# Latent attention in one block: a written-out order, one weight split per pair of heads, and a rotation in three operations

## The chip, the cores and the metric

The kernel runs on one core of a Trainium2 chip. The metric is the device time of one execution in microseconds; the time before is the median of three runs. A core has TensorE (matrix products, into PSUM), VectorE, ScalarE, GpSimd and SyncE, each with a queue of its own that it works off in the order written into the program, and 16 DMA engines that bring the weights from HBM.

## The reference

Three blocks run one after the other on 256 tokens of width 1024: a mixer with attention and a recurrence, a neighbourhood attention with its feed-forward part, and a latent attention with a mixture of 8 experts. The change is in the latent attention of the third (16 heads, 64 plain and 32 rotated columns per query and key, 64 per value):

```python
    down = h @ w_down
    c_q = _rmsnorm(down[..., :MLA_Q_LORA]) * q_norm
    c_kv = _rmsnorm(down[..., MLA_Q_LORA:MLA_Q_LORA + MLA_KV_LORA]) * kv_norm
    k_rope = down[..., MLA_Q_LORA + MLA_KV_LORA:]
    q = (c_q @ w_uq).reshape(B, S, MLA_HEADS, MLA_NOPE + MLA_ROPE)
    kv = (c_kv @ w_ukv).reshape(B, S, MLA_HEADS, MLA_NOPE + MLA_V)
    ...
        s = (jnp.einsum('bqhd,bkhd->bhqk', qn, k_nope)
             + jnp.einsum('bqhr,bkr->bhqk', qr, k_rope)).astype(jnp.float32) * scale
        p = jax.nn.softmax(s, axis=-1).astype(v.dtype)
        return jnp.einsum('bhqk,bkhd->bqhd', p, v)
```

The rotation takes neighbouring columns x1, x2 to x1 cos - x2 sin and x1 sin + x2 cos. Afterwards `w_o` projects the heads' output (the output projection, `out_proj`), a router follows, and then the experts.

## The kernel before

**Precision by splitting.** A matrix operand is split into a high part, which ScalarE casts (`whi`, line 98; `hi` in `split_to`, line 524), and a rest, which VectorE subtracts (`wlo`, line 99; `lo`). TensorE multiplies high by high, high by rest and rest by high: three matmuls for each product (lines 486, 487 and 489 for token-major products, 699 to 701 for scores). I call the subtractions rests. The turned softmax weights and the values are not split (line 676).

**The weight stream.** `Stream` brings raw weights by DMA from SyncE's queue (line 79) into a ring of buffers and splits them (`split`) up to five pieces ahead of their use. `W.next()` hands out the next piece and first splits as many further ones as there is room for.

**The latent attention.** The 16 heads are worked in eight pairs, 0 to 7. For every second pair `prepare` first forms the queries of four heads, a group (twelve matmuls of 384 columns, into two PSUM buffers `pb`), copies them (`qt`, line 1149) and rotates their last 32 columns (`turn`, lines 1068 to 1073, for each half `t` of the tokens). For each pair it then forms the keys (three matmuls of 256 columns, lines 1153 to 1155), transposes the queries (line 1162) and splits both. `scores` multiplies into PSUM buffers `pa`, one for each half of the tokens, both heads side by side. `softmax_rows` takes the maximum (line 643), scales it (644), lets ScalarE exponentiate with the row sums (646), and normalises (648, 650). `turn_P` transposes the weights of a pair (663) and ScalarE copies them back to SBUF (`pt`, 669); `pv` multiplies them with the values (676) and splits the result into `oT`, of which `out_proj` needs one piece of 128 columns for each pair.

**What sets the order.** The program is written pair by pair (`attention`, with preparation two pairs ahead), and a scheduler then lays out each engine's queue by its priorities; instructions of neighbouring pairs, and of the output projection behind them, move between each other. Only in the experts' stage is the written order kept: `in_order` chains the instructions of TensorE, ScalarE and VectorE there. The time of each stage can be read from the timeline: the attention's lead begins near 698 us, its first reduction is at 713, the output projection ends at 783, the experts' first product is at 806.

Of the kernel before, what the change touches and what calls it, by code (L numbers as in the profile page):

```python
# [9 lines left out]
F32 = mybir.dt.float32  # L10
# [4 lines left out]
OP = mybir.AluOpType  # L15
# [13 lines left out]
class Stream:  # L29
# [115 lines left out]

    def flush(self):
# [28 lines left out]
def consts():  # L175
# [8 lines left out]
    rope = np.stack([np.cos(ang), np.sin(ang)], 1).astype(np.float32)  # L184
# [4 lines left out]
def model(ctx: ExitStack, tc: tile.TileContext, A, out, cap=128):  # L189
# [443 lines left out]
    def softmax_rows(Ps, srcs, biases, scale):  # L633
# [4 lines left out]
        for i in range(n):  # L638
            if biases is not None:
                V.tensor_tensor_reduce(Ps[i], srcs[i], biases[i], scale=1.0, scalar=-3.0e38, op0=OP.add, op1=OP.max,  # L640
                                       accum_out=mx[:, i:i + 1])
            else:
                V.tensor_reduce(mx[:, i:i + 1], srcs[i], axis=AX.X, op=OP.max)
        V.tensor_scalar(mx, mx, -scale, None, OP.mult)
        for i in range(n):
            SC.activation(Ps[i], srcs[i] if biases is None else Ps[i], AF.Exp, bias=mx[:, i:i + 1], scale=scale,
                          accum_out=sums[:, i:i + 1])
# [7 lines left out]

    def turn_P(P, pt, causal, rev):
        for h in range(2):
            ps = pbc()
            p3 = ps.rearrange("p (k t n) -> p k t n", k=2, t=2)
            for kt in range(2):  # L660
                for t in range(2):
                    if not (causal and kt > t):
                        PE.transpose(p3[:, kt, t], P[:, t, h, kt * 128:(kt + 1) * 128], ident)
            run = lambda o, i: (o.rearrange("p (m n) -> p m n", n=rev), back(i, rev)) if rev else (o, i)
            if causal:
                V.tensor_copy(*run(pt[:, h, 0], ps[:, 0:256]))
                V.tensor_copy(*run(pt[:, h, 1, 128:256], p3[:, 1, 1]))
            else:
                SC.copy(*run(pt[:, h].rearrange("p k n -> p (k n)"), ps))
# [382 lines left out]
    with ExitStack() as ph:  # L1052
# [5 lines left out]
        rope = p.tile([128, 2, 2, 16], F32, name="rope")  # L1058
# [487 lines left out]
```

## Time and profile before

| | |
|---|---|
| median of three runs | 1327.18 us (1326.76 to 1331.44) |
| the profiled execution | 1326.26 us, span 1324.4 us |
| TensorE | busy 1254.7 us, 95% |
| VectorE | busy 1076.9 us, 81% |
| ScalarE | busy 846.5 us, 64% |
| DMA | 359.56 MB, mean 271 GB/s |

The span is what the profiler's records cover; the execution's own time is 1.9 us longer. A matmul's recorded time overlaps the next one's, so a busy TensorE need not be one at its peak. An engine's idle time costs only where the chain that ends last passes through it.

### The profile page before, as it was taken

The page shows a single profiled execution, that of the slowest core. Times are in us where ns is not written, and L with a number is a line of the kernel's source. Part 1 is how long each engine was busy: PE and PEld are TensorE (multiplying, and loading weights), DVE is VectorE, ACT ScalarE, POOL GpSimd, SP SyncE. Part 2 cuts the span into 40 slices and gives each one's busy share as a digit, 9 for nine tenths or more (in the row PEclk, how much of TensorE's full clock was granted, in tenths as well). Part 3 has the DMA queues.
Part 4 walks back from the last instruction along what each step waited for, and adds up shares of the span by engine and source line. Part 5 has one row for each costly group of instructions (what it writes and reads, how often), then busy time and mean ns, then how long its engine had stood idle before and what let it go on. Part 6 is the DMA issues. An engine that isn't in the chain of part 4 may idle for free. (4 is left out here: it accounts for less than half of the span.)

```text
span 1324.4 us, 20099 instructions
## 1 busy us (share of the span) xinstructions
PE 1254.7 (95%) x7459; PEld 1118.0 (84%) x7459; DVE 1076.9 (81%) x1761; ACT 846.5 (64%) x1354; POOL 37.0 (3%) x68
## 2 busy tenths in 40 slices
PE   6988999999999989999998988999999999999985
PEld 6976989999798779999987667899999889988873
DVE  6796799997897496878768867988888898888976
ACT  7874456555566453434447747788778777878762
POOL 4000000000100000000000020000000000000100
PEclk9988999999899989999979998999999999999987
DMA  9844599892785287899642145999999999999980
GB/s 330 305 143 148 159 384 343 295 315 96 231 259 163 80 307 262 312 382 346 221 138 92 32 138 192 389 372 361 368 385 366 352 381 363 370 357 391 375 320 34
DMA packets 190171, 359.56 MB, mean 271 GB/s; under 512 B 15460, under 2 KB 147970, under 8 KB 189937
## 3 DMA queue, kind: packets, MB, share of 16 engines
q1 hardware_dynamic: 187361, 351.70, 75.1%
q10 hardware_dynamic: 1584, 3.91, 0.8%
q0 software_dynamic: 1120, 2.58, 0.5%
q8 instruction: 61, 1.00, 0.3%
q14 instruction: 45, 0.37, 0.1%
HBM read 351.56 MB, written 7.06 MB: 271 GB/s over the span
## 5 line engine op out<-in xcount | busy, mean ns | idle before, releaser
L99 DVE TENSOR_TENSOR wlo<-raw,whi 128x1024 fp32r<-128x1024 f32 (+2 forms) x577 | 644.5, 1155 | 126.0 <-ACT whi L98 119.0
L98 ACT CAST whi<-raw 128x1024 fp32r<-128x1024 f32 (+2 forms) x577 | 557.7, 1003 | 115.9 <-PE pa L489 30.8
L1467 PE MATMUL pa<-whi,xT 128*128 128x448 f32 x512 | 189.3, 370 | 3.8 <-ACT whi L98 3.8
L1468 PE MATMUL pa<-wlo,xT 128*128 128x448 f32 x512 | 187.0, 365 | 1.7 <-DVE wlo L99 1.7
L1469 PE MATMUL pa<-whi,xT 128*128 128x448 f32 x512 | 186.0, 363 | 0.0
L289 DVE SCALAR_TENSOR_TENSOR acc<-raw,cact,acc 128x1024 f32<-128x1024 f32 x84 | 107.2, 1276 | 2.9 <-DMA raw<-in_w_ada_dram 2.7
L1467 PEld LDWEIGHTS pa<-whi,xT 128*128 128x128 f32 x512 | 96.7, 189 | 11.9 <-ACT whi L98 4.9
L1468 PEld LDWEIGHTS pa<-wlo,xT 128*128 128x128 f32 x512 | 96.8, 189 | 9.4 <-DVE wlo L99 3.1
L1469 PEld LDWEIGHTS pa<-whi,xT 128*128 128x128 f32 x512 | 96.5, 189 | 6.4
L486 PE MATMUL pb<-whi,hTh 128*128 128x512 f32 x224 | 88.4, 395 | 0.7 <-ACT hTh L524 0.7
L487 PE MATMUL pb<-wlo,hTh 128*128 128x512 f32 x224 | 88.4, 395 | 0.1
L478 PE MATMUL pb<-hTh,whi 128*128 128x256 f32 x512 | 74.6, 289 | 1.1 <-ACT hTh L575 0.9
L478 PEld LDWEIGHTS pb<-hTh,whi 128*128 128x128 f32 x512 | 70.3, 196 | 6.0 <-ACT hTh L575 1.6
L478 PE MATMUL pb<-hTl,whi 128*128 128x256 f32 x512 | 72.4, 283 | 0.0
L478 PE MATMUL pb<-hTh,wlo 128*128 128x256 f32 x512 | 71.9, 283 | 0.0
L489 PE MATMUL pb<-whi,hTl 128*128 128x512 f32 x224 | 71.0, 395 | 0.0
L487 PE MATMUL pa<-wlo,fh 128*128 128x512 f32 x176 | 69.2, 393 | 0.6 <-DVE wlo L99 0.6
L486 PE MATMUL pa<-whi,fh 128*128 128x512 f32 x176 | 69.3, 394 | 0.0
L478 PEld LDWEIGHTS pb<-hTl,whi 128*128 128x128 f32 x512 | 66.3, 192 | 0.0
L478 PEld LDWEIGHTS pb<-hTh,wlo 128*128 128x128 f32 x512 | 66.1, 192 | 0.0
L478 PE MATMUL pc<-hTh,whi 128*128 128x256 f32 x448 | 63.8, 285 | 1.2 <-ACT whi L98 1.2
L478 PE MATMUL pc<-hTh,wlo 128*128 128x256 f32 x448 | 63.0, 283 | 0.0
(433 smaller groups left out, 2074.0 us busy)
## 6 DMA issues: line engine op xcount, KB each, us to landing
raw<-in_moe_w_gu_dram SPq DMA_DIRECT2D x128, 896.0 KB, 7.4
raw<-in_moe_w_down_dram SPq DMA_DIRECT2D x56, 1024.0 KB, 6.7
raw<-in_w_ada_dram SPq DMA_DIRECT2D x48, 1024.0 KB, 7.8
raw<-in_w_up_dram SPq DMA_DIRECT2D x22, 1024.0 KB, 9.7
raw<-in_ffn_w_gu_dram SPq DMA_DIRECT2D x22, 1024.0 KB, 6.2
raw<-in_na_w_qkv_dram SPq DMA_DIRECT2D x12, 1024.0 KB, 5.1
raw<-in_w_down_dram SPq DMA_DIRECT2D x11, 1024.0 KB, 4.8
raw<-in_ffn_w_down_dram SPq DMA_DIRECT2D x11, 1024.0 KB
```

The source lines that it names most:

```text
L98: self.last = self.nc.scalar.copy(h, src)
L99: self.nc.vector.tensor_sub(l, src, h.bitcast(F32))
L289: V.scalar_tensor_tensor(ada_acc[0], raw, cact[:, k:k + 1], ada_acc[0], op0=OP.mult, op1=OP.add)
L478: PE.matmul(ps, lhsT=w[:, k], rhs=x[:, k], start=n + k == 0, stop=n == 2 and k == KD - 1)
L486: PE.matmul(acc[t][j][:, :n], lhsT=xh, rhs=ws[j][0], start=first, stop=False)
L487: PE.matmul(acc[t][j][:, :n], lhsT=xh, rhs=ws[j][1], start=False, stop=False)
L489: PE.matmul(acc[t][j][:, :n], lhsT=xl, rhs=ws[j][0], start=False, stop=last)
L1467: PE.matmul(ps, lhsT=xh, rhs=wh, start=k == 0, stop=False)
L1468: PE.matmul(ps, lhsT=xh, rhs=wl, start=False, stop=False)
L1469: PE.matmul(ps, lhsT=xl, rhs=wh, start=False, stop=k == KD - 1)
```

## The change

Four things change, all in the latent attention.

- **The order.** `attention` gives way to `pairs`, whose body is written in the order in which the queues are to run and is chained by `in_order`. In step `i` the scores of pair `i` for the first half of the tokens come first, then the transposes of pair `i - 1`, then the second half's scores; then the preparation of pair `i + 2`, the normalising of the second half, the rests, and the value product of pair `i - 1`. The turned weights are copied back into the tile they came from.
- **The splits.** `queries` takes a weight without splitting ahead; `Stream.one` splits one piece at the end of each step, if there is room.
- **The rotation.** The table holds cos twice and -sin, sin alternately; `turn` multiplies the columns by the one, the swapped columns by the other, and adds, for both halves of the tokens and four heads at a time. GpSimd widens the table once (`rope4`).
- **The scale.** The factor 96 ** -0.5 goes into the query split, and one reduction with a sign change covers both heads; the instruction that scaled the maxima is gone.

```diff
+    def one(self):
+
+        if self.done < len(self.items) and self.made - self.popped < self.bufs - 1:
+            self.prep()
...
-    rope = np.stack([np.cos(ang), np.sin(ang)], 1).astype(np.float32)
+    rope = np.stack([np.repeat(np.cos(ang), 2, -1), np.stack([-np.sin(ang), np.sin(ang)], -1).reshape(S, 32)], 1)
+    rope = rope.astype(np.float32)
...
+    def turn_head(P, pt, h, causal, rev, bank):
+        ps = bank()
+        p3 = ps.rearrange("p (k t n) -> p k t n", k=2, t=2)
+        for kt in range(2):
+            for t in range(2):
+                if not (causal and kt > t):
+                    PE.transpose(p3[:, kt, t], P[:, t, h, kt * 128:(kt + 1) * 128], ident)
...
+        else:
+            SC.copy(pt[:, h], ps.rearrange("p (k n) -> p k n", k=2))
...
+        rope4 = p.tile([128, 2, 4, 32], F32, name="rope4")
+        rt4 = p.tile([128, 2, 2, 4, 32], F32, name="rt4")
...
-        SC.dma_start(rope, A["c_rope"].rearrange("(t p) u f -> p t u f", p=128))
+        SC.dma_start(rope, A["c_rope"].rearrange("(t p) u f -> p u t f", p=128))
+        GP.tensor_copy(rope4, rope[:, 1, :, None, :].to_broadcast([128, 2, 4, 32]))
...
-        def turn(x, n, t, tmp):
-
-            x1, x2 = x[:, :, 0::2], x[:, :, 1::2]
-            cs, sn = (rope[:, t, u][:, None, :].to_broadcast([128, n, 16]) for u in range(2))
-            V.tensor_mul(tmp[:, 0], x1, cs)
-            V.tensor_mul(tmp[:, 1], x2, sn)
-            V.tensor_mul(tmp[:, 2], x1, sn)
-            V.tensor_mul(tmp[:, 3], x2, cs)
-            V.tensor_sub(x1, tmp[:, 0], tmp[:, 1])
-            V.tensor_add(x2, tmp[:, 2], tmp[:, 3])
+        def turn(x, n, cs, sn, a, b):
+
+            pairs = lambda y: y.rearrange("p t n (f u) -> p (t n) f u", u=2)
+            V.tensor_mul(a, x, cs[:, :, None, :].to_broadcast([128, cs.shape[1], n, 32]))
+            V.tensor_mul(pairs(b), pairs(x)[:, :, :, ::-1], pairs(sn))
+            V.tensor_add(x, a, b)
...
+        def queries(i):
+
+            w = W.next(hold=0 if i == 0 else W.bufs)
+            acc = [[pb()], [pb()]]
+            for kk in range(2):
+                tokmm(acc, cT, kk, w, kk == 0, kk == 1, halves=1, n=384, o=kk * 384)
+            x = qt[i // 2] = q.tile([128, 2, 4, 96], F32, name="qt")
+            for t in range(2):
+                SC.copy(x[:, t].rearrange("p h n -> p (h n)"), acc[t][0][:, :384])
+            return lambda: turn(x[:, :, :, 64:96], 4, rope[:, 0], rope4, rt4[:, 0], rt4[:, 1])
...
-            if i % 2 == 0:
...
-            k = kT[i % 3]
-            for h in range(2):
-                split_to(k[0][0:64, h], k[1][0:64, h], ps[h * 64:h * 64 + 64, :256])
...
-            qT = qTs[i % 3]
-            split_to(qT[0][0:96], qT[1][0:96], pq[0:96].rearrange("p (h n) -> p h n", h=2))
-            return qT, k
...
+            k, qT = kT[i % 3], qTs[i % 3]
+            kps = [ps[h * 64:h * 64 + 64, :256] for h in range(2)]
+            p3 = pq[0:96].rearrange("p (h n) -> p h n", h=2)
+            for h in range(2):
+                SC.copy(k[0][0:64, h], kps[h])
+            SC.activation(qT[0][0:96], p3, AF.Copy, scale=96 ** -0.5)
+
+            def rests():
+                for h in range(2):
+                    V.tensor_sub(k[1][0:64, h], kps[h], k[0][0:64, h].bitcast(F32))
+                V.scalar_tensor_tensor(qT[1][0:96], p3, 96 ** -0.5, qT[0][0:96].bitcast(F32), op0=OP.mult,
+                                       op1=OP.subtract)
+            return (qT, k), rests
...
-        def softmax(i, sc, P):
-            for t in range(2):
-                softmax_rows([P[:, t, h] for h in range(2)], [sc[t][:, h * 256:(h + 1) * 256] for h in range(2)],
-                             None, 96 ** -0.5)
-
-        attention(8, prepare, scores, softmax, v, oT, q, lead=2)
...
+        def pairs():
+            qk, Ps = {}, {}
+            for i in (0, 2):
+                queries(i)()
+            for i in (0, 1):
+                qk[i], rests = prepare(i)
+                rests()
...
+                def attend(t):
+                    sc = scores(t, qk[i])
+                    V.tensor_reduce(mx[t], sc.rearrange("p (h n) -> p h n", h=2), axis=AX.X, op=OP.max, negate=True)
+                    return sc
+
+                def exps(t, sc):
+                    for h in range(2):
+                        SC.activation(P[:, t, h], sc[:, h * 256:(h + 1) * 256], AF.Exp, bias=mx[t][:, h:h + 1],
+                                      accum_out=sums[t][:, h:h + 1])
+
+                def normalise(t):
+                    V.reciprocal(sums[t], sums[t])
+                    for h in range(2):
+                        V.tensor_scalar(P[:, t, h], P[:, t, h], sums[t][:, h:h + 1], None, OP.mult)
+
+                if i < 8:
+                    s0 = attend(0)
+                    exps(0, s0)
+                if i >= 1:
+                    pt = Ps[i - 1].rearrange("p t h n -> p h t n")
+                    for h in range(2):
+                        turn_head(Ps[i - 1], pt, h, False, 0, pa)
+                if i < 8:
+                    s1 = attend(1)
+                    exps(1, s1)
+                    normalise(0)
+                rotate = queries(i + 4) if i in (0, 2) else None
+                rests = None
+                if i + 2 < 8:
+                    qk[i + 2], rests = prepare(i + 2)
+                if i < 8:
+                    normalise(1)
+                if rotate:
+                    rotate()
+                if rests:
+                    rests()
+                if i >= 1:
+                    pv(pt, v, (i - 1) * 128, oT, i - 1, False)
+                W.one()
+
+        with in_order(PE, SC, V):
+            pairs()
```

Where the change moves instructions, three places show it. **VectorE's queue, at pair 3.** The names ending in a number are buffers: `sums_8017` and `sums_8027` belong to pair 3 before, `mx_8086` and `mx_8096` are the maxima of pair 4, `h_7600` holds the key parts of a later pair, `ol` is the rest of a value product.

```order
L648 RECIPROCAL sums_8017<-sums_8017 128x2
L643 TENSOR_REDUCE mx_8086<-pa_8071 128x1
L650 TENSOR_SCALAR P_8015<-P_8015,sums_8017 128x256 x2
L648 RECIPROCAL sums_8027<-sums_8027 128x2
L524 TENSOR_TENSOR h_7600<-pb_8036,h_7600 64x256
L650 TENSOR_SCALAR P_8015<-P_8015,sums_8027 128x256 x2
L643 TENSOR_REDUCE mx_8086<-pa_8071 128x1
L643 TENSOR_REDUCE mx_8096<-pa_8078 128x1
L644 TENSOR_SCALAR mx_8086<-mx_8086 128x2
```

The same place in the changed kernel (`mx_7981`, `mx_7982`: pair 3; `mx_8050`: pair 4):

```order
L1207 TENSOR_REDUCE mx_7981<-pa_7985 128x2
L1207 TENSOR_REDUCE mx_7982<-pa_8007 128x2
L1216 RECIPROCAL sums_7983<-sums_7983 128x2
L1218 TENSOR_SCALAR P_7980<-P_7980,sums_7983 128x256 x2
L1216 RECIPROCAL sums_7984<-sums_7984 128x2
L1218 TENSOR_SCALAR P_7980<-P_7980,sums_7984 128x256 x2
L1179 TENSOR_TENSOR h_7597<-pb_8020,h_7597 64x256 x2
L1180 SCALAR_TENSOR_TENSOR h_7598<-pc_8024,h_7598 96x512
L530 TENSOR_TENSOR ol_7309<-pb_8038,oh_7308 128x256
L99 TENSOR_TENSOR wlo_8046<-raw_7618,whi_8045 128x1024
L1207 TENSOR_REDUCE mx_8050<-pa_8054 128x2
```

The next pair's first reduction stood between the first and the second normalising; now it stands behind everything of this pair, the weight split included.

**ScalarE's queue, at pair 3 of the changed kernel.** `P_7980` are its weights, `P_7889` those of pair 2.

```order
L1212 ACTIVATE P_7980,sums_7983<-pa_7985,mx_7981 128x256 x2
L671 COPY P_7889<-pa_7995 128x2x256
L671 COPY P_7889<-pa_8001 128x2x256
L1212 ACTIVATE P_7980,sums_7984<-pa_8007,mx_7982 128x256 x2
L1174 CAST h_7597<-pb_8020 64x256 x2
L1175 ACTIVATE h_7598<-pc_8024 96x512
L530 CAST oh_7308<-pb_8038 128x256
L98 CAST whi_8045<-raw_7618 128x1024
```

Before, the four exponentials of pair 3 stood together and the copies (line 669) behind them; now the copies stand between the two halves.

**TensorE's queue, at the end of the attention.** Before, the output projection's matmuls (lines 486, 487 and 489, into `pa`) stand between the last pairs' transposes and value products:

```order
L486 MATMUL pa_8398<-whi_7774,oh_7308 128x512
L487 MATMUL pa_8398<-wlo_7775,oh_7308 128x512
L489 MATMUL pa_8397<-whi_7774,ol_7309 128x512
L486 MATMUL pa_8399<-whi_7667,oh_7308 128x512
L487 MATMUL pa_8399<-wlo_7668,oh_7308 128x512
L676 MATMUL pb_8351<-pt_8338,v_7317 64x256 x4
L663 MATMUL pc_8359<-ident_115,P_8317 128x128
```

In the changed kernel they come behind (lines 492, 493 and 495 are the output projection, 682 the value product, 665 the transposes):

```order
L682 MATMUL pb_8272<-P_8179,v_7317 64x256 x4
L665 MATMUL pa_8279<-ident_115,P_8229 128x128 x4
L665 MATMUL pa_8285<-ident_115,P_8229 128x128 x4
L492 MATMUL pa_8318<-whi_7664,oh_7308 128x512
L682 MATMUL pc_8291<-P_8229,v_7317 64x256
L493 MATMUL pa_8318<-wlo_7665,oh_7308 128x512
L682 MATMUL pc_8291<-P_8229,v_7317 64x256 x3
L492 MATMUL pa_8319<-whi_7664,oh_7308 128x512
```

Two of the projection's matmuls are left ahead of the last value product's end.

## Rows read from the trace of the kernel before

**Rows 1.** Windows of three stages: PE, PEld, DVE, ACT, POOL busy, clock, DMA.
```profile
702.40:713.30 10.90, 9.14 (x63) 7.90 (x63) 9.34 (x27) 7.64 (x14) 0.73 (x2) 1.00 0.33 104
713.30:764.90 51.60, 47.63 (x305) 35.56 (x303) 41.95 (x160) 39.32 (x115) 0.00 (x0) 1.00 0.12 37
764.90:782.70 17.80, 17.80 (x80) 14.68 (x80) 7.61 (x16) 5.49 (x10) 0.65 (x3) 1.00 0.46 156
```
**Rows 2.** A window of the experts' stage, the same columns.
```profile
1000.00:1100.00 100.00, 100.00 (x506) 90.44 (x505) 86.71 (x90) 81.19 (x109) 0.00 (x0) 1.00 1.02 369
```
**Rows 3.** TensorE's timeline: start, duration, line, tiles, count, idle before and its releaser.
```profile
706.36 0.42 PE L486 MATMUL pb<-whi,cTh 128*128 128x384 f32 x1
...
755.90 0.40 PE L486 MATMUL pa<-whi,oh 128*128 128x512 f32 x1
...
763.38 1.56 PE L676 MATMUL pc<-pt,v 128*64 128x256 f32 x8
764.87 0.50 PE L486 MATMUL pa<-whi,oh 128*128 128x512 f32 x1
...
782.69 1.03 PE L1200 MATMUL pb<-ident,xres 128*128 128x128 f32 x8
```
**Rows 4.** VectorE's timeline in the stage.
```profile
713.33 1.09 DVE L643 TENSOR_REDUCE mx<-pa 128x1 f32<-128x256 f32 x3
...
749.04 0.68 DVE L524 TENSOR_TENSOR qTl<-pc,qTh 96x512 fp32r<-96x512 f32 x1
749.64 0.60 DVE L650 TENSOR_SCALAR P<-P,sums 128x256 f32<-128x256 f32 x2
...
761.08 0.17 DVE L648 RECIPROCAL sums<-sums 128x2 f32<-128x2 f32 x1 [0.85 <-ACT P L646]
761.28 0.62 DVE L650 TENSOR_SCALAR P<-P,sums 128x256 f32<-128x256 f32 x2
...
765.52 1.21 DVE L99 TENSOR_TENSOR wlo<-raw,whi 128x1024 fp32r<-128x1024 f32 x1
766.65 0.41 DVE L524 TENSOR_TENSOR ol<-pc,oh 128x256 fp32r<-128x256 f32 x1
```
**Rows 5.** VectorE's groups by line and shape, 690 to 770 us: busy, mean ns | idle before.
```profile
L1069 DVE TENSOR_TENSOR rt<-qt,rope 128x64 f32<-128x64 f32 x8 | 1.7, 216 | 0.0
...
L1097 DVE SCALAR_TENSOR_TENSOR h<-pa,ry,qn 128x256 f32<-128x256 f32 x2 | 1.0, 480 | 0.0
L524 DVE TENSOR_TENSOR cTl<-pc,cTh 128x256 fp32r<-128x256 f32 x2 | 0.8, 420 | 0.2 <-ACT cTh L524 0.2
```
**Rows 6.** The rotation table: its issue on ScalarE's queue and its first use.
```profile
669.83 0.44 ACTq L1061 DMA_DIRECT2D rope<-in_c_rope_dram  x1
...
691.57 0.17 DVE L1068 TENSOR_TENSOR rt<-h,rope 128x16 f32<-128x16 f32 x1
```
**Rows 7.** ScalarE's timeline in the stage.
```profile
747.10 0.37 ACT L524 CAST k1h<-pb 64x256 fp32r<-64x256 f32 x1 [0.18 <-PE pb L1155]
747.37 0.58 ACT L524 CAST qTh<-pc 96x512 fp32r<-96x512 f32 x1
...
760.00 0.50 ACT L646 ACTIVATE P<-pa,mx 128x256 f32<-128x256 f32 x1
...
760.46 0.50 ACT L646 ACTIVATE P<-pa,mx 128x256 f32<-128x256 f32 x1
760.81 0.23 ACT L646 ACTIVATION_READ_ACCUMULATOR P<-pa,mx 128x1 f32 x1
...
762.74 0.59 ACT L669 COPY pt<-pc 128x512 f32<-128x512 f32 x1 [1.08 <-PE pc L663]
763.22 0.59 ACT L669 COPY pt<-pb 128x512 f32<-128x512 f32 x1
```
**Rows 8.** Windows of 2 us around a pause of TensorE, the columns of rows 1.
```profile
82.00:84.00 2.00, 0.00 (x0) 0.00 (x0) 2.00 (x8) 2.00 (x7) 0.00 (x0) 1.00 0.71 205
84.00:86.00 2.00, 0.74 (x2) 0.52 (x3) 1.97 (x7) 1.18 (x2) 0.00 (x0) 0.57 0.92 318
```

More of the change, by code (lines that the diff above doesn't have):

```diff
@@ L638, in softmax_rows @@
         for i in range(n):
[L639 to L643, printed above, removed]
+            V.tensor_tensor_reduce(Ps[i], srcs[i], biases[i], scale=1.0, scalar=-3.0e38, op0=OP.add, op1=OP.max,
+                                   accum_out=mx[:, i:i + 1])
         V.tensor_scalar(mx, mx, -scale, None, OP.mult)
         for i in range(n):
-            SC.activation(Ps[i], srcs[i] if biases is None else Ps[i], AF.Exp, bias=mx[:, i:i + 1], scale=scale,
+            SC.activation(Ps[i], Ps[i], AF.Exp, bias=mx[:, i:i + 1], scale=scale,
                           accum_out=sums[:, i:i + 1])
@@ L654, in back @@
         return x.rearrange("p (m n) -> p m n", n=n)[:, :, ::-1]
+    def turn_head(P, pt, h, causal, rev, bank):
[5 more added lines that the diff above has]
+                    PE.transpose(p3[:, kt, t], P[:, t, h, kt * 128:(kt + 1) * 128], ident)
+        run = lambda o, i: (o.rearrange("p (m n) -> p m n", n=rev), back(i, rev)) if rev else (o, i)
+        if causal:
+            V.tensor_copy(*run(pt[:, h, 0], ps[:, 0:256]))
+            V.tensor_copy(*run(pt[:, h, 1, 128:256], p3[:, 1, 1]))
+        else:
+            SC.copy(pt[:, h], ps.rearrange("p (k n) -> p k n", k=2))
     def turn_P(P, pt, causal, rev):
         for h in range(2):
-            ps = pbc()
-            p3 = ps.rearrange("p (k t n) -> p k t n", k=2, t=2)
-            for kt in range(2):
-                for t in range(2):
[L662 to L669, printed above, removed]
+            turn_head(P, pt, h, causal, rev, pbc)
     def pv(pt, v, col, oT, i, causal):
@@ new lines, in prepare, with scores @@
+            return (qT, k), rests
+        def scores(t, qk):
+            (qh, ql), (kh, kl) = qk
+            ps = pa()
+            sl = slice(t * 128, (t + 1) * 128)
+            for h in range(2):
+                scores3(ps[:, h * 256:(h + 1) * 256], qh[0:96, h, sl], ql[0:96, h, sl], kh[0:96, h], kl[0:96, h])
+            return ps
+        def pairs():
[5 more added lines that the diff above has]
+                rests()
+            for i in range(9):
+                sc, mx, sums = [], [], []
+                if i < 8:
+                    P = Ps[i] = qP.tile([128, 2, 2, 256], F32, name="P")
+                    mx, sums = ([sm.tile([128, 2], F32, name=x) for _ in range(2)] for x in ("mx", "sums"))
+                def attend(t):
[15 more added lines that the diff above has]
+                    pt = Ps[i - 1].rearrange("p t h n -> p h t n")
+                    for h in range(2):
+                        turn_head(Ps[i - 1], pt, h, False, 0, pa)
[7 more added lines that the diff above has]
+                    qk[i + 2], rests = prepare(i + 2)
+                if i < 8:
+                    normalise(1)
[6 more added lines that the diff above has]
+                W.one()
```

30 lines of the change are left out of this document (7 added, 23 removed).

## The prediction

> **What bounds the kernel now.** I read the windows by stage first, because the change touches one stage of some 60 us in a run of 1324. [rows 1] holds three of them: the lead into the latent attention, its eight pairs (713.3 to 764.9 us, TensorE busy 47.6 of 51.6 us, VectorE 42.0, ScalarE 39.3), and the rest of the output projection, where TensorE never stops. The reader is to see that in the pairs no engine is idle for long and none is full. Next a window of the mixture-of-experts stage: [rows 2] has TensorE busy for all of 100 us, with the DMA engines at a share of 1.02. What comes late there is not made up, so what the attention gains or loses should reach the end of the span one for one. Then I went through each engine's timeline in the stage, for durations and for the spacing of neighbours (an instruction's successor starts before its recorded end). The sums use the spacing for the time an engine is held, and the recorded duration for what another engine waits for.
>
> The end to compare is in [rows 3]: the last value product frees TensorE at 764.87, and by then 18 of the 96 matmuls of the output projection have been done in gaps since 755.90. The other 78 take until 782.69, 0.228 us each. The first reduction of a score starts at 713.33 [rows 4]. So the old order needs 51.5 us from the first reduction to the last value product, with 4.1 us of the next stage inside.
>
> **The change part by part.** The rest of the program keeps its order, so all of the change lies between 691 and 783 us.
>
> *Small savings.* The rotation of four heads was twelve VectorE instructions of 128x64, 0.215 us long [rows 5] and some 0.14 apart, 1.6 us; now it is three of 128x256 at 0.34 (the spacing of 256 columns, from three reductions in 1.09 us [rows 4]) and 0.08 for the add's wait, 1.1 us; four times. One reduction of 512 columns takes the place of two of 256: by the 96x512 subtraction at 749.04, followed at 749.64 [rows 4], I take 0.60 held and 0.68 to its end, against 2 x 0.34. The scaling of the maxima goes, 0.15 us in the chain. In the key rotation of the lead three small instructions go twice, some 0.4 us together. The added table copy on GpSimd has from the table's issue at 669.83 to its first use at 691.57 [rows 6], which hides it; without that cover it would cost its own microsecond at the lead. In all some 4 us of VectorE work go.
>
> *The new order.* In the old order the reductions of the next pair stand between the steps of this one, so that VectorE and ScalarE have another pair's work at hand. In the new one VectorE closes a pair before the next one's first reduction: two reductions, normalise, normalise, key rests, query rest, output rest, weight split. ScalarE has two exponentials, both turned copies, two exponentials. A period is then one chain that crosses between the two engines three times. Its terms, for a pair with preparation and split:
> first reduction and the hop, 0.75; the first two exponentials hold ScalarE 2 x 0.455 = 0.91 (those at 760.00 and 760.46 [rows 7]); two turned copies 2 x 0.48 = 0.96 (those at 762.74 and 763.22 [rows 7]); the second two exponentials until their sums are there, 1.07 (760.00 to the end at 761.04, and the reciprocal at 761.08 [rows 4, 7]); reciprocal 0.20 and two scalings of 0.27, 0.74 [rows 4]; two key rests 0.68; query rest 0.66 (0.60 as a subtraction, and 10% more, as 0.480 against 0.420 in [rows 5], since it now multiplies too); output rest 0.34; split 1.13 (765.52 to 766.65 [rows 4]).
> The sum is 7.24 us, of which VectorE works 5.4. It waits 0.6 us for the first sums and 1.1 for the second with nothing else to do. ScalarE's key and query casts (at most 2 x 0.37 + 0.58 [rows 7]) end before VectorE asks. TensorE's work for a pair lies inside: 15 matmuls of 256 columns at half of 0.228, twelve transposes at no more than that, and 1.5 for the value product [rows 3], 4.6 us.
>
> The pairs then: pair 0 has no copies and no output rest yet, but a rotation: 7.24 - 0.96 - 0.34 + 1.07 = 7.0. Pairs 1 and 3: 7.24. Pair 2, with a rotation: 8.3. Pairs 4 and 5, without the split (pair 4's stands in VectorE's wait): 6.1 each. Pair 6, without rests: 4.8. Pair 7: 4.5 from reduction to scaled weights, 0.7 for transposes, 1.1 to the end of the second copy, and 1.06 from there to a free TensorE (763.22 + 0.59 = 763.81 against 764.87 [rows 3, 7]): 7.4. Together 54.2 us.
>
> *The lead.* TensorE resumes the first query product at 706.36 [rows 3]. Now both groups' products, both rotations and two pairs' rests stand ahead of the first reduction. Nine matmuls at 0.17 (0.228 x 384/512) end near 708; the second group's twelve wait for two PSUM buffers that ScalarE must empty, until 710.6; copy and rotation until 712.4; rests, 2 x 1.34, until 715.1. Less 0.4 from the shorter key rotation: 714.7, against 713.33.
>
> *The tail.* 714.7 + 54.2 = 768.9: the last value product ends 4.0 us later. Two matmuls of the output projection stand before that end now, where 18 did. Sixteen more come after it: 16 x 0.228 = 3.6 us. Together 7.6 us, on the profiled execution's own 1326.26 us 1333.9. The median of the three runs is 0.9 above that execution, the lowest 0.5; I give 1334.5.
>
> *Bounds.* No row shows a reduction of 512 columns: between 0.41 (as one of 256) and 0.75 (as two, 0.34 + 0.41) I take 0.68, the row nearest in size; over eight pairs -2.2 to +0.6 us. Three hops a pair may each cost from nothing to 0.15 us where I have some 0.05: -1 to +2.4.
>
> *TensorE's clock.* TensorE now idles in one piece, 7.24 - 4.6, some 2.5 us a pair. [rows 8] has it idle through 82 to 84 us and a mean clock of 0.57 in 84 to 86: it fell from 2.4 to 1.2 GHz after a pause of about 3 us. In the pairs as they are the clock is 1.00 [rows 1]. My pauses are shorter than the one that these rows show, and the sum stays. The Trainium skill's page "TensorE: Matmul & The Clock Gate", section "HAM oscillation — how this bites in real kernels", says that waits between bursts of matmuls can drop the clock so that every burst starts cold; by that rule the sum would be that of the clock rival below. No run here shows yet whether these pauses are long enough.
>
> **The rivals.** *The clock falls in the pairs.* At 1.2 GHz the 4.6 us of a pair become 9.2, more than the chain's 7.24; each pair that runs cold costs up to 2 us, three of them 6: 1340. For it speaks [rows 8]; against it that the pauses are shorter, and that a busy TensorE gets its clock back.
> *The chain is shorter than its terms.* If neighbours overlap more than their spacing shows, or the reduction costs as little as one of 256 columns, a pair takes 0.4 to 0.8 us less, and 3 to 6 of the 7.6 us go: 1328.5 to 1331.5. A measurement of this kernel can tell about 0.5%, 6.6 us, from no change: below 1320.5 is faster, above 1333.8 slower.
> *VectorE's two waits vanish (faster).* The place is between the second reduction and the two reciprocals, the price 0.6 + 1.1 us a pair. Were the sums there when VectorE asks, eight pairs would take 13.6 us less: 1321. The sides change where the two waits together are below 0.75 us. For it: TensorE has real idle time in the old order, since a matmul's recorded time overlaps the next one's. Against: ScalarE's order is written out, and the copies stand ahead of the second exponentials.
> *The savings decide.* If the old stage was held by VectorE's own work, 4 us less of it give 1323. Against: VectorE is idle for 9.6 of the 51.6 us [rows 1].
>
> **How the numbers follow.** The forecast has 0.62, with a range of its own of 1331 to 1338 by the bounds. The clock rival has 0.13, the shorter chain 0.15, the two on the faster side 0.10. The time is that of the likeliest, 1334.5. With about 0.1 left out at each end the range is 1328 to 1341. Slower by over 0.5%: seven tenths of the forecast's 0.62 and the clock's 0.13, 0.57. Faster by over 0.5%: most of the 0.10, 0.07. The rest, 0.36, lies within.
>
> **What would show it.** VectorE idle ahead of the reciprocals, some 1.7 us a pair, released by the exponentials. First reductions 7.2 us apart with a split, 6.1 without, 8.3 where a rotation stands. The first reduction near 714.7, the last value product ending near 769, then 94 matmuls without a gap, and an experts' stage of the same length. Wrong would be: pairs less than 6 us apart, a clock below 1.00 in them, or a lead that ends before 713.

## The result and the profile after

The changed kernel takes 1340.88 us (median of 5, 1338.84 to 1344.77), against 1327.18 before: ratio 1.0100, 95% interval 1.0083 to 1.0117. It is slower by 13.7 us, 6.4 above the forecast of 1334.5 and 0.12 below the upper end of the stated range. The profiled execution took 1340.99 us, 14.7 more than that of the kernel before.

First the stage in windows, in the columns of [rows 1]: the lead to the first reduction, the pairs, the rest of the output projection.

```profile
707.20:720.40 13.20, 10.85 (x69) 8.97 (x69) 7.50 (x19) 6.90 (x14) 0.73 (x2) 1.00 0.05 19
720.40:775.90 55.50, 43.74 (x283) 33.66 (x281) 41.08 (x101) 38.99 (x114) 0.00 (x0) 0.94 0.16 50
775.90:797.30 21.40, 21.40 (x95) 17.67 (x95) 7.56 (x16) 6.66 (x11) 0.63 (x3) 1.00 0.39 130
```

The lead takes longer, the pairs 55.5 us instead of 51.6 with TensorE busy for 43.7 instead of 47.6 of them and a mean clock of 0.94, and TensorE then works 21.4 us without a gap instead of 17.8. Next TensorE's timeline, with the events of [rows 3]; the first row is the start of the query down product, where both kernels have the same work behind them but for the edit of the rotation table.

```profile
687.40 0.50 PE L492 MATMUL pa<-whi,hTh 128*128 128x160 f32 x1
...
711.16 0.42 PE L492 MATMUL pb<-whi,cTh 128*128 128x384 f32 x1
...
774.86 1.08 PE L682 MATMUL pc<-P,v 128*64 128x256 f32 x6
775.87 0.50 PE L492 MATMUL pa<-whi,oh 128*128 128x512 f32 x1
...
797.31 1.04 PE L1263 MATMUL pb<-ident,xres 128*128 128x128 f32 x8
```

In the kernel before the same product starts here:

```profile
682.62 0.50 PE L486 MATMUL pa<-whi,hTh 128*128 128x160 f32 x1
```

That is 4.78 us earlier, though ahead of it only the rotation table's load and copy are edited; the difference is there by 342 us (the same rest of a cast stands at 341.78 before and at 346.56 after). From this start to the end of the output projection the kernel before needs 100.07 us and the changed one 109.91, 9.84 more; 4.78 and 9.84 make the 14.7. Last, VectorE in pair 1, from its first reduction to that of pair 2, as in [rows 4]:

```profile
727.66 1.28 DVE L1207 TENSOR_REDUCE mx<-pa 128x2 f32<-128x512 f32 x2
729.43 0.17 DVE L1216 RECIPROCAL sums<-sums 128x2 f32<-128x2 f32 x1 [0.49 <-ACT P L1212]
...
731.32 0.17 DVE L1216 RECIPROCAL sums<-sums 128x2 f32<-128x2 f32 x1 [1.07 <-ACT P L1212]
731.52 0.62 DVE L1218 TENSOR_SCALAR P<-P,sums 128x256 f32<-128x256 f32 x2
732.05 0.85 DVE L1179 TENSOR_TENSOR k0l<-pb,k0h 64x256 fp32r<-64x256 f32 x2
732.93 0.69 DVE L1180 SCALAR_TENSOR_TENSOR qTl<-pc,qTh 96x512 fp32r<-96x512 f32 x1
733.54 0.41 DVE L530 TENSOR_TENSOR ol<-pb,oh 128x256 fp32r<-128x256 f32 x1
733.87 1.21 DVE L99 TENSOR_TENSOR wlo<-raw,whi 128x1024 fp32r<-128x1024 f32 x1
735.00 1.28 DVE L1207 TENSOR_REDUCE mx<-pa 128x2 f32<-128x512 f32 x2
```

These rows show the chain of the forecast: two waits for the exponentials, 0.49 and 1.07 us, and a period of 7.34.

For each kernel below the same marks were read from its profile; ratios further down are to runs of the kernel before made beside it. Lead is from the query down product's start to the first reduction; pairs, to the matmul that follows the last value product; rest, to the end of the output projection. One of experiment 6's six runs took 1574.11 us at a mean clock of 0.738, and its median is that of the other five.

| kernel | product starts | lead | pairs | rest | stage | median, us (runs) |
|---|---|---|---|---|---|---|
| before | 682.62 | 30.71 | 51.54 | 17.82 | 100.07 | 1327.18 (3) |
| changed | 687.40 | 33.06 | 55.41 | 21.44 | 109.91 | 1340.88 (5) |
| 1 scheduler's order | 683.19 | 33.93 | 45.19 | 20.55 | 99.67 | 1327.84 (12) |
| 2 rotation only | 686.73 | 30.94 | 54.83 | 17.82 | 103.59 | 1330.87 (12) |
| 3 next pair first | 685.81 | 33.10 | 63.70 | 21.46 | 118.26 | 1350.67 (5) |
| 4 one query group in the lead | 685.76 | 31.25 | 60.49 | 21.45 | 113.19 | 1345.44 (6) |
| 5 waits filled | 684.82 | 35.57 | 51.89 | 21.48 | 108.94 | 1338.20 (6) |
| 6 banks of the last pairs | 682.97 | 33.06 | 55.87 | 18.32 | 107.25 | 1336.66 (5) |
| 7 matmuls added | 684.38 | 33.08 | 58.05 | 21.48 | 112.61 | 1340.86 (6) |
| 8 changed, again | 682.87 | 35.58 | 56.48 | 21.44 | 113.50 | 1341.69 (6) |
| 9 scheduler and banks | 688.82 | 33.75 | 46.69 | 17.81 | 98.25 | 1327.84 (12) |
| 10 the same, later group | 682.60 | 32.13 | 45.61 | 17.81 | 95.55 | 1326.45 (12) |
| 11 first rows first | 683.20 | 33.80 | 57.63 | 21.44 | 112.87 | 1339.91 (6) |
| 12 written order, three edits | 685.12 | 32.55 | 51.58 | 17.81 | 101.94 | 1330.29 (12) |

### The profile page after: what moved, and what is told of

Its sections match the earlier page's. It is cut to its first block, busy times and chain, and to the rows that moved or that the text cites. A ratio compares the mean times of both kernels' runs of the same rounds, so it can differ in the third digit from the quotient of the medians.

```text
span 1339.1 us, 20034 instructions
## 1 busy us (share of the span) xinstructions
PE 1259.5 (94%) x7459; PEld 1122.4 (84%) x7459; DVE 1074.5 (80%) x1687; ACT 846.9 (63%) x1354; POOL 37.1 (3%) x69
```

## The experiments

The theory is that of the forecast: the written order makes a pair one chain between VectorE and ScalarE, and moves lead and tail. The rivals are that the new operations or banks cost, and that TensorE's clock costs.

**1. The scheduler's order.**
```diff
-        with in_order(PE, SC, V):
-            pairs()
+        pairs()
```


> The changed kernel with its written order of the pairs given back to the scheduler; every instruction stays (three-operation rotation, one reduction per score tile, turning in place). If the written order is what costs (a chain that crosses between VectorE and ScalarE three times a pair), the scheduler brings the next pair's reductions between the steps again: first reductions of neighbouring pairs come closer than 7.2 us, and the time falls to 1323 to 1330. If the new operations or the shared banks cost, and not their order, it stays at 1336 or more.

Measured: 1327.84 us, ratio 1.0002 (0.9990 to 1.0013). The same instructions without the written order are as fast as the kernel before, so taken as a whole the loss is the order's, and not that of the new operations. The pairs need only 45.2 us, 6.4 less than before:

```profile
717.10:762.40 45.30, 42.92 (x284) 32.68 (x283) 35.91 (x97) 35.93 (x111) 0.00 (x0) 0.98 0.08 27
```

VectorE works 35.9 us in them instead of 42.0 [rows 1], and TensorE's share is 42.9 of 45.3. What the lighter work gives in the pairs goes again in the lead (+3.2) and in the tail (+2.7, 90 matmuls behind the last value product instead of 78). So lead and tail are long under the scheduler too (33.93 and 20.55, against 33.06 and 21.44 in the changed kernel): what the written order itself costs lies in the pairs, 55.41 us against 45.19.

**2. The rotation alone, on the kernel before.**
```diff
-                    tmp = q.tile([128, 4, 4, 16], F32, name="rt4")
-                    turn(qt[0][:, t, :, 64:96], 4, t, tmp)
+                turn(qt[0][:, :, :, 64:96], 4, rope[:, 0], rope4, rt4[:, 0], rt4[:, 1])
```


> The kernel before with nothing but the three-operation rotation (and its table). If the order is the cause, this gives a microsecond or two at most: 1325 to 1327.5, not to be told from before. If the rotation itself is the loss (the swapped read of the second multiplication, the table copy on GpSimd), it is above 1330.

Measured: 1330.87 us, ratio 1.0021 (1.0010 to 1.0032): above what the theory gave, and just into the rival's side. The loss of 3.5 us in the stage lies in the pairs (54.83), not in the lead, where the rotation first stands (30.94). Since the same rotation is in experiment 1, with pairs of 45.19, the operation itself doesn't cost. The profile shows where most of it went: the same 305 matmuls as in [rows 1] keep TensorE busy for 50.37 us instead of 47.63, since the clock stood at 0.50 twice, from 723.6 to 727.0 and from 750.9 to 754.3 us.

```profile
717.70:772.50 54.80, 50.37 (x305) 38.74 (x304) 40.65 (x133) 39.74 (x115) 0.00 (x0) 0.94 0.11 34
```

Why it fell there was not tried. The merged rotation waits for both copies of a group, so that the scheduler takes other steps next; whether that makes the pauses is only argued.

**3. The next pair's first scores ahead.** In a pair the order is now: turned tiles, second scores, first normalisation, then
```diff
+                if i < 7:
+                    attend(i + 1, 0)
                 if i < 8:
                     normalise(i, 1)
...
                 if i >= 1:
                     pv(pt, v, (i - 1) * 128, oT, i - 1, False)
...
                     qk[i + 2], rests = prepare(i + 2)
+                W.one()
...
                 if rests:
                     rests()
-                W.one()
```


> The changed kernel, order alone edited: the next pair's first score tile, its reduction and its exponentials stand ahead of this pair's second normalisation, and output rest and split ahead of the key and query rests. By the chain theory VectorE's two waits (0.5 and 1.07 us a pair) are filled, a pair with a split takes about 5.6 us and one without 4.9 instead of 7.3 and 6.3, the last value product ends some 10 us earlier, and the time is 1329 to 1333. If it is TensorE's clock that holds the pairs, the waits move to the scores and the time stays above 1337.

Measured: 1350.67 us, ratio 1.0176 (1.0157 to 1.0195), 10 us worse than the changed kernel. VectorE's rows around pair 2 and TensorE's beside them:

```profile
734.05 0.42 DVE L530 TENSOR_TENSOR ol<-pb,oh 128x256 fp32r<-128x256 f32 x1 [0.91 <-ACT oh L530]
736.99 1.23 DVE L99 TENSOR_TENSOR wlo<-raw,whi 128x1024 fp32r<-128x1024 f32 x1 [2.52 <-ACT whi L98]
...
739.64 0.68 DVE L1206 TENSOR_REDUCE mx<-pa 128x2 f32<-128x512 f32 x1
```

```profile
738.59 0.38 PE L706 MATMUL pa<-k0l,qTh 96*128 96x256 f32 x1 [1.41 <-DVE k0l L1179]
739.77 0.38 PE L707 MATMUL pa<-k0h,qTl 96*128 96x256 f32 x1 [0.79 <-DVE qTl L1180]
```

The wait for the sums is gone, but the split now waits 2.52 us for its cast, and the rests stand behind the split. The cast stands on ScalarE behind the key and query casts, these wait for TensorE's preparation, that stands behind the next pair's scores, and those wait for the rests of the pair before (1.41 and 0.79 us). I had closed a longer ring than the one opened: the second reductions of pairs 0 to 4 come 9.3 to 10.8 us apart. By its words the expectation came out on the clock's side: the waits moved to the scores, and the time is above 1337. But VectorE's rests end these waits, not slow matmuls. The clock did stand at 0.50 three times in the pairs of this profile, 6.8 us each, and what that adds isn't separated. So the run decides nothing between chain and clock; it shows the price of one misplaced step in a written order.

**4. One query group in the lead.**
```diff
-            for i in (0, 2):
-                queries(i)()
+            queries(0)()
...
-                rotate = queries(i + 4) if i in (0, 2) else None
+                rotate = queries({0: 2, 1: 4, 3: 6}[i]) if i in (0, 1, 3) else None
```
(and in pair 0 the preparation of pair 2 comes behind the rotation and the split)

> The changed kernel with one query group instead of two ahead of the first reduction; the other groups follow in pairs 0, 1 and 3. If the lead was lengthened by the second group's 12 matmuls (2.1 us) and its rotation (1.2 us), the first reduction comes about 3 us earlier after the start of the query down product, one more rotation (1.2 us) stands inside the pairs, and the time is 1338 to 1340. If the lead is held by something else, it stays at 1341.

Measured: 1345.44 us, ratio 1.0124 (1.0104 to 1.0144). The lead is 1.8 us shorter, where about 3 were expected, but pair 0 now takes 9.85 us instead of 7.20:

```profile
724.23 1.22 DVE L99 TENSOR_TENSOR wlo<-raw,whi 128x1024 fp32r<-128x1024 f32 x1 [2.57 <-ACT whi L98]
...
726.86 1.27 DVE L1205 TENSOR_REDUCE mx<-pa 128x2 f32<-128x512 f32 x2
```

Pair 2's preparation waits for the rotation inside the pair, and VectorE stands 2.57 us. So the second group has a use in the lead: there its rotation is done before pair 2's preparation asks for it.

**5. Two instructions moved into VectorE's waits.**
```diff
                     attend(i, 1)
+                    if ol:
+                        ol()
                     normalise(i, 0)
+                    if split:
+                        split()
...
-                    pv(pt, v, (i - 1) * 128, oT, i - 1, False)
-                W.one()
+                    ol = pv_late(pt, i - 1)
+                split = W.one_late()
```
(`pv_late` and `one_late` issue all but the subtraction, and return it)

> The changed kernel with two VectorE instructions of a pair deferred into the waits of the next one: the output rest (0.34 us) between the second reduction and the first reciprocal, where VectorE waits 0.5, and the weight split's subtraction (1.13 us) between the two normalisations, where it waits 1.07; its cast stays where it was. If the chain of a pair is what sets the pace, a period falls from 7.2 to about 5.9 us with a split and from 6.3 to 5.9 without, some 6 us in all, and the time to 1333 to 1336. If VectorE's own work or TensorE sets it, first reductions stay 7.2 us apart and the time stays within 2 us of the changed kernel's.

Measured: 1338.20 us, ratio 1.0062 (1.0043 to 1.0082). Pair 2 of it:

```profile
733.52 0.41 DVE L1251 TENSOR_TENSOR ol<-pb,oh 128x256 fp32r<-128x256 f32 x1
734.15 0.17 DVE L1240 RECIPROCAL sums<-sums 128x2 f32<-128x2 f32 x1 [0.22 <-ACT P L1236]
...
734.88 1.22 DVE L174 TENSOR_TENSOR wlo<-raw,whi 128x1024 fp32r<-128x1024 f32 x1
736.04 0.17 DVE L1240 RECIPROCAL sums<-sums 128x2 f32<-128x2 f32 x1
```

In the same pair of the changed kernel VectorE waited 0.55 and 1.06 us; the first wait has shrunk to 0.22 and the second is gone; pairs 0 and 1 take 6.06 and 5.87 us instead of 7.20 and 7.34, the pairs together 51.89 instead of 55.41. So the chain sets the pace of the written order there. Of the 6 us expected 3.5 came: pair 4 now takes 7.04 us instead of 6.26, as two splits stand between its normalisations, and pair 6 5.75 instead of 4.83, as VectorE waits 1.22 us for scores while the clock is at 0.50. The time falls by 2.7 us only, above the 1333 to 1336 expected; in this profile the clock stood at 0.50 in the lead, which took 35.57 (see 8). Two of the six runs took 1333.7 and 1333.9 us, the other four 1338.2 to 1339.3.

**6. Other banks for the last two pairs.**
```diff
-                    sc = scores(t, qk[i])
+                    sc = scores(t, qk[i], pa if i < 7 else pbc)
...
-                        turn_head(Ps[i - 1], pt, h, False, 0, pa)
+                        turn_head(Ps[i - 1], pt, h, False, 0, pa if i < 7 else pbc)
```


> The changed kernel with the last pair's score tiles and the last two pairs' turned tiles in the four small-pool PSUM banks, so that the four large ones are free for the output projection's sums a pair earlier. If the 16 matmuls that moved behind the last value product were held back by these banks, a good part of them comes forward again: the last value product ends where it did, 78 to 85 matmuls follow it instead of 94, and the time is 2 to 4 us less, 1336.5 to 1339. If something else held them, no change.

Measured: 1336.66 us, ratio 1.0067 (1.0050 to 1.0084). The output projection starts inside pair 6 again:

```profile
760.89 0.50 PE L492 MATMUL pa<-whi,oh 128*128 128x512 f32 x1 [1.73 <-ACT P L1212]
...
771.90 0.74 PE L495 MATMUL pa<-whi,ol 128*128 128x512 f32 x2
```

16 of its matmuls stand ahead of the last value product's end, 80 behind, and the rest falls from 21.44 to 18.32 us. So the last pairs' tiles in the large pool's banks had held back 14 of the 16 matmuls. Score tiles and turned tiles moved together here, and which of them holds is not separated.

**7. Matmuls added in TensorE's wait.**
```diff
+                    if i < 8:
+                        ps = pbc()
+                        for _ in range(12):
+                            PE.matmul(ps[:, :256], lhsT=wn[0][:, i * 128:(i + 1) * 128], rhs=cT[0][:, 2], start=True,
+                                      stop=True)
-                    pv(pt, v, (i - 1) * 128, oT, i - 1, False)
+                    pv(pt, v, (i - 1) * 128, oT, i - 1, False, ps if i < 8 else None)
```


> The changed kernel with twelve matmuls of 256 columns (1.4 us at the full clock) added ahead of each value product but the last, into its own bank and overwritten by it, where TensorE waits 2.2 us for the turned copies. If the fallen clock in two of the pairs costs nothing because the chain between VectorE and ScalarE hides it, the time stays at 1339 to 1342. If the clock is where the part of the loss went that the chain does not explain (some 4 us), the clock in the pairs is 1.00 and the time 1336 to 1338.

Measured: 1340.86 us, ratio 1.0096 (1.0079 to 1.0113). The mean clock rises from 0.966 to 0.971 and the time doesn't move. But the clock still fell once, in pair 2, so the test doesn't price it cleanly:

```profile
736.12 0.64 PE L1168 MATMUL pb<-ident,qt 128*96 128x128 f32 x4 [2.68 <-ACT qt L1156]
736.51 2.20 PE L1245 MATMUL pc<-cTh,wnh 128*128 128x256 f32 x12
```

```profile
741.07 0.42 DVE L530 TENSOR_TENSOR ol<-pc,oh 128x256 fp32r<-128x256 f32 x1 [1.89 <-ACT oh L530]
```

TensorE had paused 2.68 us for the query copies, ran the added matmuls and the value product at 0.50, and VectorE waited 1.89 for the output rest: pair 2 took 11.15 us. In the other pairs, 7.21 to 7.41 us with a split and 6.26 or 6.27 without, the added work is hidden entirely.

**8. The changed kernel once more.**

> The changed kernel once more, unedited. In its first profile the query down product began 4.8 us later than in that of the kernel before, although nothing ahead of it differs. If that is chance of the execution, this profile has it at 683 to 685 and the median of these runs is nearer 1337; if it belongs to the program, it is again near 687 and the median at 1341.

Measured: 1341.69 us, ratio 1.0108 (1.0085 to 1.0131). Neither half of the expectation came as written. The query down product starts at 682.87, as in the kernel before: the 4.78 us were chance, and over the fourteen profiles this start lies anywhere between 682.60 and 688.82, in an order of its own. Yet the time is no lower, since the stage now took 113.50 us. The clock shows where:

```profile
704.00:706.00 2.00, 1.35 (x11) 1.35 (x12) 0.56 (x3) 0.85 (x2) 0.00 (x0) 0.92 0.00 0
706.00:708.00 2.00, 2.00 (x10) 1.99 (x10) 0.30 (x2) 1.01 (x2) 0.00 (x0) 0.50 0.03 8
712.00:714.00 2.00, 1.96 (x10) 1.64 (x9) 0.60 (x2) 0.67 (x2) 0.00 (x0) 0.87 0.00 0
```

```profile
704.65 0.44 PE L1107 MATMUL pc<-ident,h 128*128 128x128 f32 x2 [1.20 <-DVE h L1102]
704.93 2.73 PE L1140 MATMUL pc<-acc,ones 128*128 128x8 f32 x16
707.51 0.67 PE L492 MATMUL pb<-whi,cTh 128*128 128x384 f32 x1
```

In the lead the clock fell to 0.50, 1.2 GHz, for nearly 7 us, behind a pause of 1.20 us and while sixteen matmuls of 8 columns ran. At the same place, with the same pause, the first profile has 1.00, and the sixteen take 1.85 us instead of 2.73:

```profile
709.18 0.44 PE L1107 MATMUL pc<-ident,h 128*128 128x128 f32 x2 [1.20 <-DVE h L1102]
709.46 1.85 PE L1140 MATMUL pc<-acc,ones 128*128 128x8 f32 x16
```

Here TensorE's query products are the path, and the lead grows from 33.06 to 35.58. The same lead stands in six profiles (the changed kernel's and those of experiments 3, 5, 6, 7 and 8): in two of them the clock fell in it, and it took 35.57 and 35.58, in the other four 33.06 to 33.10. The second place is pair 2, first in this profile, then in the first one:

```profile
737.08 1.09 PE L1168 MATMUL pb<-ident,qt 128*96 128x128 f32 x4 [2.65 <-ACT qt L1156]
```

```profile
739.10 0.64 PE L1168 MATMUL pb<-ident,qt 128*96 128x128 f32 x4 [1.11 <-ACT qt L1156]
```

VectorE's waits in the second profile:

```profile
740.53 0.42 DVE L530 TENSOR_TENSOR ol<-pc,oh 128x256 fp32r<-128x256 f32 x1 [0.38 <-ACT oh L530]
741.47 1.23 DVE L99 TENSOR_TENSOR wlo<-raw,whi 128x1024 fp32r<-128x1024 f32 x1 [0.52 <-ACT whi L98]
```

After a pause of 2.65 us the transposes and the value product ran at half the clock, output rest and split waited 0.38 and 0.52, and the pair took 9.63 us instead of 8.56. In the first profile the clock had fallen one pair earlier, TensorE came to this place later, and the pause was 1.11 us with the clock at 1.00 behind it. Experiment 6 repeats that (a fall in pair 1, a pause of 1.09, 8.55 us for pair 2); experiment 11 repeats the other (none in pair 1, a pause of 2.66 and a fall in pair 2, 9.42 us). What a fall costs depends on the pair in which it comes.

**9 and 10. The scheduler's order with the banks of experiment 6, and with the second group written later.** Experiment 9 is 1 and 6 together; 10 has in addition
```diff
-            for i in (0, 2):
-                queries(i)()
+            queries(0)()
             for i in (0, 1):
                 qk[i], rests = prepare(i)
                 rests()
+            queries(2)()
```


> The changed kernel with the scheduler's order (as in the first experiment) and the small-pool banks for the last two pairs (as in the sixth). In the first experiment 90 matmuls of the output projection stood behind the last value product, here 78 as in the kernel before. If the two effects add, 12 x 0.228 = 2.7 us less than the first experiment's 1327.84: about 1325. If the scheduler had already used those gaps for other work, 1327 to 1328.

> As the ninth, and the second query group is written behind the preparation of the first two pairs, so that the first pair's work has the older place in the scheduler's list. The first reduction came 33.9 us after the start of the query down product in the first experiment, against 30.7 in the kernel before. If the second group ahead of it is why, it comes at about 31 here and the time is 1 to 3 us under the ninth's, 1322 to 1324. If that group is needed just as early by pair 2, the gain is given back there and the time equals the ninth's.

Measured: 1327.84 us for 9, ratio 0.9990 (0.9975 to 1.0004), and 1326.45 for 10, ratio 0.9981 (0.9967 to 0.9994). In 9 the rest shrinks by the 2.74 us expected, to 17.81, while the pairs take 1.5 more and the median is that of experiment 1; its runs scatter from 1322.14 to 1330.84, and whether it gained stays open. In 10 the stage is 95.55 us, 4.5 under the kernel before:

```profile
714.70:760.40 45.70, 44.20 (x300) 34.38 (x298) 38.60 (x101) 37.39 (x113) 0.00 (x0) 1.00 0.14 41
760.40:778.20 17.80, 17.80 (x80) 14.69 (x80) 6.40 (x15) 5.49 (x10) 0.63 (x3) 1.00 0.47 156
```

The first reduction comes 32.13 us after the product's start, later than the 31 expected, and TensorE is busy for 44.2 of 45.7 us in the pairs. It is the only version faster than both kernels, by 0.2%, less than its profile's 4.5 us promise. In the profiled execution 2.1 of these 4.5 were lost behind the stage: from the end of the output projection to the end of the span it has 543.77 us, the kernel before 541.71, with one stretch of 2.20 us near the end of its last chain for which the profile shows no cause (experiment 3 has one of 1.76). The median of its runs, 1326.45, is another 2.6 us above that execution, and no profile shows why.

**11. The first 128 tokens first.**
```diff
-            for kk in range(2):
-                tokmm(acc, cT, kk, w, kk == 0, kk == 1, halves=1, n=384, o=kk * 384)
+            for ts in ((0,), (1,)) if i == 0 else ((0, 1),):
+                for kk in range(2):
+                    tokmm(acc, cT, kk, w, kk == 0, kk == 1, ts=ts, halves=1, n=384, o=kk * 384)
```


> The changed kernel with one edit in the lead: the first query product takes all of the first 128 tokens before the second 128, so that six of its matmuls instead of three stand ahead of TensorE's wait for the second latent half (as the kernel before has it). The wait falls from 1.2 to 0.7 us. If the clock's fall in the lead (0.50 over some 5 us in two of the profiles of the written order, 2.5 us of time) follows that wait and the sixteen narrow matmuls behind it, the first reduction comes 33 us or less after the start of the query down product and the median is 1337.5 to 1339.5. If the fall comes anyway, the median is 1340 to 1341.

Measured: 1339.91 us, ratio 1.0082 (1.0067 to 1.0098). The wait is as expected, and the clock falls all the same:

```profile
704.97 0.44 PE L1107 MATMUL pc<-ident,h 128*128 128x128 f32 x2 [0.67 <-DVE h L1102]
...
708.32 0.34 PE L495 MATMUL pb<-whi,cTl 128*128 128x384 f32 x1
708.49 0.42 PE L492 MATMUL pb<-whi,cTh 128*128 128x384 f32 x1
708.71 0.52 PE L493 MATMUL pb<-wlo,cTh 128*128 128x384 f32 x1
709.03 0.52 PE L495 MATMUL pb<-whi,cTl 128*128 128x384 f32 x1
```

The pause is 0.67 us, and from 708.7 the matmuls of 384 columns stand 0.32 apart instead of 0.17. So the clock can fall here without the longer pause; in experiment 12, with the same edit, it doesn't. What makes it fall stays open. The median lies just below the 1340 to 1341 expected for this case.

**12. The written order with edits 5, 6 and 11.**

> The written order with the edits of the fifth (two VectorE instructions in the waits), the sixth (banks of the last pairs) and the eleventh together. If chain, tail and lead are separate costs, their gains add: about 3.5 + 4 + 2 under the changed kernel's 1341, 1331 to 1333, still above the kernel before. If they are one cost seen three times, it stays at 1336 or above.

Measured: 1330.29 us, ratio 1.0020 (1.0008 to 1.0032), 10.6 under the changed kernel, a little more than the 1331 to 1333 expected. In its stage the clock is 1.00 throughout:

```profile
717.60:769.30 51.70, 43.71 (x299) 34.00 (x297) 42.09 (x102) 39.90 (x115) 0.00 (x0) 1.00 0.17 54
```

Its rest is that of the kernel before and its pairs too (51.58); what is left is a longer lead (32.55 against 30.71). Against the changed kernel's profile the pairs gain 3.8 us and the rest 3.6, in experiments 5 and 6 alone 3.5 and 3.1: chain and tail are separate costs that add.

## Why the prediction was right or wrong

**The chain: right.** The forecast's spacings of first reductions were 7.0, 7.24, 8.3, 7.24, 6.1, 6.1 and 4.8 us, with 7.4 for the last pair; the first profile has 7.20, 7.34, 8.56, 7.39, 6.26, 6.26, 4.83 and 7.57, 55.4 us against 54.2. The two waits, forecast at 0.6 and 1.1, are 0.5 and 1.07. Experiment 1 shows that the order is the cause of the longer pairs, 5 that these waits are in the chain. Of the 1.2 us too much the largest part is one term: the two key rests hold VectorE for 0.88 us (732.05 to 732.93), where 0.68 was taken, in six pairs; the query rest holds it for 0.61 instead of 0.66.

**The tail: right.** Forecast were 94 matmuls and 3.6 us; the rest grew by 3.62. Experiment 6 shows the banks to be what moved 14 of the 16, and experiment 9 the same for 12 under the scheduler (90 to 78): this cost belongs to the banks and not to the written order.

**The lead: mechanism right, mis-sized.** The term gave +1.4 us; the first profile has +2.35. Less the 4.78 of the later start, the second group's products end at 710.8 (forecast 710.6) and its rotation at 712.7 (712.4). The rests of two pairs take 2.99 us instead of 2.68, by the same key rests. The 0.4 us that the shorter key rotation should save don't arrive: the first query product resumes 23.76 us after the down product's start, before it was 23.74.

**TensorE's clock: wrong.** The step that failed is "My pauses are shorter than the one that these rows show, and the sum stays." The clock fell in every profile of the written order but that of experiment 12, here after a pause of 2.25 us in pair 1 of the first profile. The pause of [rows 8], read as about 3 us, lasted 4.18 (to 85.26 us), and said nothing of shorter ones:

```profile
729.93 2.46 PE L682 MATMUL pb<-P,v 128*64 128x256 f32 x8 [2.25 <-ACT P L671]
```

```profile
728.00:730.00 2.00, 0.07 (x1) 0.07 (x2) 1.48 (x5) 1.62 (x6) 0.00 (x0) 1.00 0.51 113
730.00:732.00 2.00, 2.00 (x8) 0.88 (x8) 0.90 (x4) 1.95 (x8) 0.00 (x0) 0.60 0.92 346
```

So came a sign that the forecast had named as wrong, a clock below 1.00 in the pairs. The clock rival was right that it falls and wrong on the price. In the first profile it stood at 0.50 from 730.4 to 733.8 and from 754.3 to 757.7 us, in pairs 1 and 4, and they took 7.34 and 6.26 us like their neighbours: the chain hid it. It is paid where TensorE is the path: 2.5 us in the lead and 1.07 in pair 2 in the second profile. It isn't the written order's alone: in the profiles of experiments 1 and 9 it fell once, around the first reduction. The Trainium skill's page "TensorE: Matmul & The Clock Gate", section "HAM oscillation — how this bites in real kernels", says that waits between bursts of matmuls can drop the clock, so that every burst starts cold. The traces agree with that only in part: two falls in the pairs of either profile, and the full clock after the other pauses.

**The sum.** Lead, pairs and rest give 2.35 + 3.87 + 3.62 = 9.84 us in the first profile and 4.87 + 4.94 + 3.62 = 13.43 in the second, against 7.6 forecast. The medians differ by 13.7, and in the runs beside experiment 8 by 14.0 (1341.69 against 1327.74). Of the second sum 7.6 are the forecast's terms, 2.2 the mis-sized ones, and 3.6 the clock, 2.5 in the lead and 1.1 in pair 2. That most executions are like this one is not shown: the clock fell in this lead in two of six profiles. That the median came inside the stated range is luck: 1340.88 is 0.12 us under its end, experiment 8's 1341.69 is over it, and the forecast's own range ended at 1338. The clock rival's 1340 is near by luck as well, since its three pairs at 2 us each did not come. The first execution reached a like time with a shorter stage by the chance of the 4.78 us ahead of it. The forecast "an experts' stage of the same length" held: from the end of the output projection to the end of the span it is 541.71 us before and 541.79 after. Over the fourteen profiles it lies between 541.4 and 543.8, so a gain of a microsecond or two in the attention can't be followed to the end in one execution.

## What to carry to other kernels

Before an order is written out over a scheduler's, list for each engine what stands between an instruction and the one whose result it waits for: here the same lighter work made the pairs 6.4 us shorter in the scheduler's order (2.7 of them moved behind the last value product) and 3.9 longer in a written one. Waits in such a chain are filled by deferring the subtractions that nobody needs yet, and the banks of the last pairs decide when the next product may begin. A move that fills one wait can close a longer ring of waits, as experiment 3 did, so follow the ring through every engine's queue before running it.

## What was not expected of the hardware

The clock of one program falls at different places in different executions. With the same instructions and the same pause of 1.20 us in the lead, one execution of the changed kernel has a granted clock of 1.00 there and another 0.50 for nearly 7 us. Where it fell in pair 1, the pause in pair 2 was 1.1 us instead of 2.65 and the clock stayed up behind it. And work with no edit near it takes a different time from one profile to the next: 682.60 to 688.82 us to the start of the query down product.
